# Three reorderings in a fused GLA and MLA block: gate sums behind the sixth product, two weight splits sooner, the last head's outputs ahead of the first pair's values

## The chip, the cores and the metric

The kernel runs on one core of a Trainium2 chip. The metric is the device time of one execution in microseconds (us), lower is better. The core has five instruction queues that run on their own and wait for each other by semaphores: TensorE (PE, matmuls; PEld is its loading of weights), VectorE (DVE), ScalarE (ACT), GpSimd (POOL) and SyncE (SP, which here only issues DMAs). Each works through its instructions strictly in order: what stands behind a waiting instruction waits too.

## The reference, cut to what matters

One transformer block over 512 tokens of width 1024, in fp32. One wide projection feeds a gated linear attention (GLA, 4 heads, two directions, chunks of 64) and a latent attention (MLA, 8 heads); both are gated, added, projected, and followed by a squared-ReLU MLP.

```python
n = rmsnorm(h, g_mix[l])
proj = n @ w_in[l]
(gq, gk, gv, gr, z_gf, z_gb, cq, ckv, kr, z_ma, z_mb) = jnp.split(proj, SPLIT_IDX, axis=-1)
y_gla = gla_branch(gq, gk, gv, gr, z_gf, z_gb, w_gate_f[l], b_gate_f[l], w_gate_b[l], b_gate_b[l], g_gla[l])
y_mla = mla_branch(cq, ckv, kr, positions, g_q[l], w_uq[l], g_kv[l], w_ukv[l])
merged = jax.nn.sigmoid(z_ma) * y_gla + jax.nn.sigmoid(z_mb) * y_mla
h = h + merged @ w_out[l]
m = rmsnorm(h, g_mlp[l])
h = h + jnp.square(jax.nn.relu(m @ w_ff1[l])) @ w_ff2[l]
return rmsnorm(h, g_final)
```

z_gf and z_gb (16 columns each) are the inputs of the GLA's two forget gates, kr (32 columns) is the rotated part of the MLA's key, z_mb gates the MLA.

## The kernel before, in words

**Split numbers.** Every product is made in fp32r from operands split into a high and a low half: ACT copies the operand into the rounded type (high, L93), DVE subtracts it from the operand (low, L94), and `mm3` (L87 to L90) issues three matmuls, high by high (L88), high by low (L89) and low by high (L90). Here "gk1h" and "gk1l" are the halves of the weights for gk of head 1. The halves of weights live in pools of four buffers each (tags wh and wl, L213 to L216), so a split writes into the buffer of the fourth split ahead of it and waits until PE has read that. PSUM has two pools of four banks, "mm" and "at" (L77).

**The order of the work.** Up to L1076 (PE: L1077) the order on each engine is the order in which the program issues its instructions (`in_program_order`); behind that a list scheduler orders them, held only by `goes_behind`, which puts the first instruction of one traced stretch behind the last of another on the named engines.

**Products by seven (L586 to L666).** The projections gr and gv (1024 columns each) are made as seven products of half blocks instead of eight, in the order SEVEN = (1, 2, 5, 6, 3, 7, 4). Products 1, 6, 7 and 4 add onto the same two accumulators ("grx", "gvx"), 5 and 3 onto another two ("grz", "gvz"), 2 has its own ("gvw"). Between them ACT copies partial results (L655) or DVE adds them (L658). So after the sixth product of gr (number 7) DVE adds its accumulators to grc, and the seventh (number 4) goes on adding onto them. The loop at L983 walks through the steps of gr and then gv; each step also prepares the weights two steps ahead (right sums at L603, then the split), and for some steps a filler is run behind the product: another small projection.

**The gate inputs.** The filler of step (0, 6), the fourth product of gr, is `z_chunk_run` (L407 to L423): 16 matmuls give z_gf, z_gb and kr in the bank "zk", with the product by the low halves in other partitions. Then the sums: ACT copies half of the bank (L415), DVE adds (L416) and scales into kr (L417), ACT and DVE split the gate inputs into z4 (L418 to L420), and SP issues four copies that build kr and kswap (L421 to L423). z4 is read by `Gates(0)` (L436), behind gv's third product; kr and kswap by `rotary_k` (L826), far behind.

**The stretch behind gr (L1017 to L1041)** is written out by hand: the gate logs, sums and exponentials of head 0 (`Gates`) between gv's last products, then gk of head 1 (`begin_qk(1, 1)` splits its weights, `finish_qk` makes the product), then gv's last product and the gate zb5 (`begin(C_ZB + 5 * P, "zb5")` splits, `finish_zb` makes the product). `gv.sinks(3)` and `gv.sinks(7)` split rows of v (L679, helper L97 and L98).

**The last GLA head and the first pair (L1115 to L1119).** `up_units(0)` (L846) makes the query, key and value of the first two MLA heads: it yields behind the weights, behind uq, behind uk and behind each of two value blocks uv. Then `gla_out` (L692) makes the last GLA head's outputs, 48 matmuls into two "at" banks, `gla_squares` (L707) their squares on ACT and their scale on POOL, `gla_gated` (L717) the gated rows on DVE (L722), which frees the banks. The attention loop (L1122) runs over 32 tiles of scores: scores s (L905), row maximum top (L907), exponential e (L910), scaling by the reciprocal of the sum (L911 to L915), the flip tp on PE (L924), the values av; the next pair's units are strewn among them.

Of the kernel before, what the change touches and what calls it, by code (L numbers as in the profile page):

```python
# [18 lines left out]
P = 128  # L19
# [16 lines left out]
C_ZA, C_ZB = 3776, 4800  # L36
# [20 lines left out]
def tile_block(ctx: ExitStack, tc: tile.TileContext, t, out: bass.AP):  # L57
# [10 lines left out]
    def u2(name, dt=F32, shape=(P, S)):  # L68
        return tl(list(shape), dt, "u2", 29, name)
# [37 lines left out]
    def traced():  # L107
        return len(nc.cur_bb.bb.instructions)
# [12 lines left out]
    PE_ONLY = (mybir.EngineType.PE,)  # L121
    SPLITTERS = (mybir.EngineType.Activation, mybir.EngineType.DVE)

    def goes_behind(late, early, engines):

        ins = nc.cur_bb.bb.instructions
        for e in engines:
            a, b = [[i for i in ins[x:y] if i.engine == e] for x, y in (early, late)]
            if a and b:
                issued_after(b[0], a[-1].name)  # L130
# [259 lines left out]
    def split_gates():  # L390
        for d in ("f", "b"):
            nc.scalar.activation(gates[d], wg_raw[d], AF.Copy)
            nc.vector.tensor_tensor(
                gates[d][64:128, :], wg_raw[d][64:128, :], raw(gates[d][64:128, :]), op=ALU.subtract
            )
# [11 lines left out]
    def z_chunk_run(begun):  # L407
        w, acc = begun
        for k in range(KD):
            for x in range(2):  # L410
                nc.tensor.matmul(
                    acc, w[:, k, :], xT[k][:, x, :], start=k == 0 and x == 0, stop=k == KD - 1 and x == 1
                )
        both = u2("zkl")
        nc.scalar.activation(both[0:64, :], acc[64:128, :], AF.Copy)  # L415
        nc.vector.tensor_tensor(both[0:64, :], acc[0:64, :], both[0:64, :], op=ALU.add)  # L416
        nc.vector.tensor_tensor(kr[0:64, :], both[0:64, :], R[0:64, :], op=ALU.mult)  # L417
        nc.scalar.activation(z4[0:32, :], kr[0:32, :], AF.Copy)  # L418
        nc.vector.tensor_tensor(z4[32:64, :], kr[0:32, :], raw(z4[0:32, :]), op=ALU.subtract)
        nc.vector.tensor_copy(z4[64:128, :], raw(z4[0:64, :]))  # L420
        for a, b in ((32, 48), (48, 32)):  # L421
            nc.sync.dma_start(kswap[a + 32 : a + 48, :], kr[b : b + HALF, :])
            nc.sync.dma_start(kr[a + 32 : a + 48, :], kr[a : a + HALF, :])  # L423
# [268 lines left out]
    def gla_out(h, sc):  # L692

        half, at = h // 2, (h % 2) * GDV
        accs = [ps("at", f"gla{h}o{j}") for j in range(2)]
        c = slice(at, at + GDV)
        os = []
        for i in range(NT):
            o = accs[i // 2][:, (i % 2) * GDV : (i % 2 + 1) * GDV]
            tok = slice(i * P, (i + 1) * P)  # L700
            for j in range(NT):
                mm3(o, sc[j][:, 0, tok], sc[j][:, 1, tok], v[j, half][:, 0, c], v[j, half][:, 1, c],
                    j == 0, j == NT - 1)
            os.append(o)
        return os
# [36 lines left out]
    class Latent:  # L742
# [4 lines left out]
        def begin(self, j):  # L747
            self.begun[j] = proj_begin(w_in, self.col + j * P, f"{self.name}{j}")
# [97 lines left out]
    def up_units(pr):  # L846

        wq = stage(3, P, f"wq{pr}")
        for k in range(3):
            nc.sync.dma_start(  # L850
                wq[:, k, :].rearrange("p (h e) -> p h e", h=2), w_uq[:, k, 2 * pr : 2 * pr + 2, 0:NOPE]
            )
        wqh, wql = halves(3, P, f"wq{pr}")
        split(wqh, wql, wq, nc.gpsimd)
        wk = stage(2, 384, f"wk{pr}")
        nc.sync.dma_start(
            wk.rearrange("p k (h e) -> p k h e", h=2), w_ukv[:, :, 2 * pr : 2 * pr + 2, :]
        )
        wh, wl = halves(2, 384, f"wk{pr}")
        src = wk.rearrange("p k (h e) -> p k h e", h=2)  # L860
        for k in range(2):
            for c, e in ((slice(0, 128), slice(0, NOPE)), (slice(128, 384), slice(NOPE, 192))):
                split(wh[:, k, c].rearrange("p (h e) -> p h e", h=2),
                      wl[:, k, c].rearrange("p (h e) -> p h e", h=2), src[:, k, :, e], nc.gpsimd)
        qs = []
        for i in range(2):
            q = u4(f"q{pr}{i}")
            h = (2 * pr + i) * HALF
            for x in range(2):
                at = NOPE + x * HALF  # L870
                nc.sync.dma_start(raw(q[at : at + HALF]), raw(ro[x][h : h + HALF]))
            qs.append(q)
        yield
        accq = up_T(wqh, wql, cq, f"uq{pr}")
        for i in range(2):
            split_scaled(qs[i][0:64, 0, :], qs[i][0:64, 1, :], accq[i * 64 : i * 64 + 64, :], QK_SCALE)
        yield
        acck = up_T(wh[:, :, 0:128], wl[:, :, 0:128], ckv, f"uk{pr}")
        for i in range(2):
            kb = kbuf[2 * (pr % 2) + i]  # L880
            split(kb[0:64, 0, :], kb[0:64, 1, :], acck[i * 64 : i * 64 + 64, :])
        yield
        vs = []
        for j in range(2):
            acc = ps("mm", f"uv{pr}{j}")
            for i in range(2):
                tok = slice((2 * j + i) * P, (2 * j + i + 1) * P)
                for k in range(2):
                    mm3(acc[:, i * 256 : i * 256 + 256], ckv[k][:, 0, tok], ckv[k][:, 1, tok],
                        wh[:, k, 128:384], wl[:, k, 128:384], k == 0, k == 1)  # L890
            hl = u4(f"v{pr}{j}", F32R, (P, 2, 2, 256))
            split(hl[:, 0].rearrange("p a b -> p (a b)"), hl[:, 1].rearrange("p a b -> p (a b)"), acc)
            vs.append(hl)
            yield
        for i in range(2):
            heads[2 * pr + i] = (qs[i], kbuf[2 * (pr % 2) + i], vs, slice(i * MV, (i + 1) * MV))
# [63 lines left out]
    def begin_qk(h, x):  # L960
        col, name = ((C_GQ, "gq"), (C_GK, "gk"))[x]
        return begin(col + h * P, f"{name}{h}")
# [4 lines left out]
    def finish_zb(f, begun):  # L967
# [3 lines left out]
    fillers = {  # L971
        (0, 2): (lambda: begin(C_ZB + 4 * P, "zb4"), lambda w: finish_zb(4, w)),
        (0, 6): (lambda: z_chunk_begin("mm"), z_chunk_run),
        (1, 2): (lambda: begin_qk(1, 0), lambda w: finish_qk(1, 0, w)),
    }
# [6 lines left out]
    begun = {}  # L982
    for n, (a, m) in enumerate(steps[:-4]):  # L983
        ahead = steps[n + 2]
        if a == 0:
            for x in {3: (0,), 7: (2, 1), 4: (3,)}.get(m, ()):
                sevens[1].load(x)
        if steps[n + 1] in fillers:
            at = traced()
            begun[steps[n + 1]] = fillers[steps[n + 1]][0]()  # L990
            goes_behind((at, traced()), loading, (mybir.EngineType.SP,))
        if n == 1:
            split_sums(x_y, 5, 6)
        if n == 2:
            split_sums(x_z, 7, 3)
        if (a, m) == (0, 5):
            load_gates()
            pos_i = u2("pos_i", I32)
            nc.gpsimd.dma_start(pos_i, t["positions"][0].partition_broadcast(P))
        if (a, m) == (0, 4):  # L1000
            split_gates()
        if (a, m) in fillers:
            sevens[a].product(m)
            sevens[ahead[0]].prepare(ahead[1])
            fillers[a, m][1](begun.pop((a, m)))
        elif m == 7:
            sevens[a].multiply(m)
            sevens[ahead[0]].prepare(ahead[1])
            sevens[a].sinks(m)
        else:  # L1010
            sevens[ahead[0]].prepare(ahead[1])
            sevens[a].product(m)
# [13 lines left out]
    gate.sums("b")  # L1026
    gv.right_sums(4)
    gv.right_split(4, 0)
    gate.exps("b")
    gv.multiply(3)  # L1030
    w_k = begin_qk(1, 1)
    gv.multiply(7)
    near, nxt, far = gla_qk(0, gate.parts)
    gv.right_split(4, 1)
    gv.sinks(3)
    gv.sinks(7)
    w_b = begin(C_ZB + 5 * P, "zb5")
    finish_qk(1, 1, w_k)
    gv.product(4)
    w_a = begin_za(0)  # L1040
# [2 lines left out]
    for h in range(GH - 1):  # L1043
        sc = gla_scores(near, nxt, far)
        gate = Gates(h + 1)
        gate.logs()
        w_b = begin_za(2 * h + 1)
        acc = proj_run(w_a, xT)
# [10 lines left out]
        os = gla_out(h, sc)  # L1059
# [3 lines left out]
        if h < 2:  # L1063
            w_b = begin_qk(h + 2, 1)
# [14 lines left out]
    h = GH - 1  # L1079
# [16 lines left out]
    sc = gla_scores(near, nxt, far)  # L1096
# [3 lines left out]
    at = traced()  # L1100
# [8 lines left out]
    at = traced()  # L1109
# [2 lines left out]
    ro = rotary_q()  # L1112
    goes_behind((mid, traced()), (at, mid), PE_ONLY)
    g2.append(gated(proj_run(zb, xT, None, range(3, KD)), "b7")[1])
    for _ in up_units(0):  # L1115
        pass
    os = gla_out(h, sc)
    rs = gla_squares(h, os)
    gla_gated(h, os, rs)  # L1119
    LAG_B, LAG_C = 3, 6  # L1120
    units = iter(())
    for n in range(4 * MH + LAG_C):  # L1122
        if n % 8 == 1 and n // 8 + 1 < MH // 2:
            units = up_units(n // 8 + 1)
# [107 lines left out]
    begun = rows_product(merged, t["w_out"][0], KD, "wo", first_half_square, normed, flipped)  # L1232
# [256 lines left out]
```

## Time and profile before

| | |
|---|---|
| median of 3 timed runs | 776.53 us (776.03 to 777.01) |
| profiled execution, its own time | 774.47 us |
| its span, first to last instruction | 772.8 us |
| granted TensorE clock, mean | 0.998 |
| instructions | 10152 |
| POOL busy | 117.9 us of the span |
| moved by DMA | 73.94 MB, mean 96 GB/s |

The span is what the trace covers; the profiled execution's own time is 1.67 us longer than it. Lines of the profile name the line of the kernel, the engine, the operation and the tiles (out<-in). In a timeline the first column is the start in us from the span's beginning, the second the duration (for a row "x2" from the first start to the last end), and the bracket at the end is the engine's idle time ahead of the instruction and what ended it. Matmuls overlap: each shows 0.39 us though the next starts earlier, so a loss on PE is read from the distance of starts. In a row of busy time by stretch stand the stretch, its length, then busy time and count of PE, PEld, DVE, ACT and POOL, the granted clock, the DMA engines' share and GB/s. In the list of the costliest groups, after the bar, stand busy time, mean ns of one, and idle time ahead.

### The profile page before, as it was taken

To read this page: it belongs to the slowest core of one execution; us is meant where nothing else is said; L and a number is where in the kernel's file an instruction comes from. 1 tells how busy PE (TensorE), PEld (TensorE's weight loads), DVE (VectorE), ACT (ScalarE), POOL (GpSimd) and SP (SyncE) were. 2 spreads that over 40 slices of the span, in tenths; PEclk is the share of its full clock that TensorE was granted. 3 is DMA by queue.
4 is the path that set the end of the run, shared out by engine and by line. 5 is a ranking of instruction groups with operands and counts; after the bars stand their busy time and mean duration, and the time that the engine had idled before them with its cause. 6 is when DMAs were issued, how large, how long until landed. Compare 5 with 4: busy or idle time off the path is not lost.

```text
span 772.8 us, 10152 instructions
## 1 busy us (share of the span) xinstructions
PE 759.4 (98%) x3768; PEld 640.6 (83%) x3768; DVE 571.3 (74%) x850; ACT 441.8 (57%) x749; POOL 117.9 (15%) x190
## 2 busy tenths in 40 slices
PE   9999899999999999999999999999999999999996
PEld 7888687888898889899888988888888888888885
DVE  7788989665667775899963676965787478848695
ACT  7556657384566555788833465444644465336644
POOL 0710004251615105211110100000000000000014
PEclk9999999999999999999999999999999999999999
DMA  9732301221324516131033731263115510560002
GB/s 315 244 110 82 119 24 28 56 56 55 82 56 103 91 33 150 35 82 55 29 144 101 250 106 55 68 203 111 55 38 182 160 31 28 176 179 1 27 1 109
DMA packets 93185, 73.94 MB, mean 96 GB/s; under 512 B 15088, under 2 KB 74480, under 8 KB 93136
## 3 DMA queue, kind: packets, MB, share of 16 engines
q1 hardware_dynamic: 92048, 70.14, 30.9%
q10 hardware_dynamic: 864, 2.38, 0.8%
q0 software_dynamic: 224, 0.79, 0.3%
q8 instruction: 29, 0.48, 0.3%
q14 instruction: 20, 0.16, 0.1%
HBM read 69.62 MB, written 2.10 MB: 93 GB/s over the span
## 4 chain that ended last, share of the span: by engine, by line
PE 90%; DVE 5%; ACT 2%; issue 1%; POOL 1%; POOLq 0%; ACTq 0%
PE f L89 8%; PE f L88 8%; PE f L90 8%; PE gx L88 4%; PE gx L89 4%; PE gx L90 4%; PE first L325 3%; PE za L88 2%; PE wo L90 2%; PE za L89 2%; PE wo L88 2%; PE gz L88 2%; PE za L90 2%; PE wo L89 2%; PE gz L89 2%; PE gz L90 2%
## 5 line engine op out<-in xcount | busy, mean ns | idle before, releaser
L1428 POOL DMA_DIRECT2D gfin<-in_g_final x1 | 0.7, 653 | 282.7 <-PE f L90 282.7
L1253 DVE TENSOR_TENSOR w<-w,w 128x1024 f32<-128x1024 f32 x32 | 38.7, 1220 | 0.4
L907 DVE TENSOR_REDUCE top<-s 128x1 f32<-128x512 f32 x32 | 21.7, 679 | 5.2 <-PE s L90 5.1
L910 ACT ACTIVATE e<-s,top 128x512 f32<-128x512 f32 x32 | 21.9, 686 | 5.6 <-DVE top L907 2.9
L470 POOL COPY v3f<-rrf 128x4 f32<-128x4 f32 x4 | 2.8, 708 | 140.3 <-DVE rrf L453 140.3
L1200 DVE TENSOR_TENSOR h<-gx,h 128x512 f32<-128x512 f32 x32 | 21.5, 683 | 1.9 <-PE gx L90 1.8
L94 DVE TENSOR_TENSOR pT<-tp,pT 128x512 fp32r<-128x512 f32 x32 | 21.6, 678 | 0.8 <-ACT pT L93 0.7
L93 ACT ACTIVATE pT<-tp 128x512 fp32r<-128x512 f32 x32 | 19.0, 595 | 4.0 <-PE tp L924 3.8
L942 POOL TENSOR_TENSOR tb<-tb,za 128x512 f32<-128x512 f32 x8 | 11.2, 1402 | 54.8 <-DVE tb L941 40.5
L924 PE MATMUL tp<-ident,e 128*128 128x128 f32 x128 | 19.2, 272 | 0.0
L88 PE MATMUL av<-pT,v 128*128 128x256 f32 x64 | 19.1, 299 | 0.0
L89 PE MATMUL av<-pT,v 128*128 128x256 f32 x64 | 18.5, 289 | 0.0
L1306 ACT ACTIVATE fa<-f 128x512 f32<-128x512 f32 x32 | 18.5, 577 | 0.0
L924 PEld LDWEIGHTS tp<-ident,e 128*128 128x128 f32 x128 | 15.5, 140 | 3.5 <-PE s L90 0.6
L90 PE MATMUL av<-pT,v 128*128 128x256 f32 x64 | 18.2, 285 | 0.0
L93 ACT ACTIVATE gbh<-y 128x512 fp32r<-128x512 f32 x16 | 10.1, 634 | 14.0 <-DVE y L1323 14.0
L94 DVE TENSOR_TENSOR sc<-sc,sc 128x512 fp32r<-128x512 f32 x16 | 10.9, 690 | 9.5 <-ACT sc L93 9.5
L93 ACT ACTIVATE sc<-sc 128x512 fp32r<-128x512 f32 x16 | 9.3, 595 | 11.5 <-DVE sc L541 11.5
L88 PE MATMUL s<-kbuf,q 96*128 96x512 f32 x32 | 14.0, 437 | 1.2 <-DVE grb L722 0.9
L93 ACT ACTIVATE b_10h<-w 128x1024 fp32r<-128x1024 f32 x7 | 7.4, 1060 | 12.1 <-PE gz L90 6.0
L93 ACT ACTIVATE b_20h<-w 128x1024 fp32r<-128x1024 f32 x7 | 7.4, 1059 | 12.1 <-PE gz L90 6.0
L93 ACT ACTIVATE b_00h<-w 128x1024 fp32r<-128x1024 f32 x7 | 7.4, 1057 | 12.1 <-PE gz L90 6.0
(1569 smaller groups left out, 2885.7 us busy)
## 6 DMA issues: line engine op xcount, KB each, us to landing
w<-in_w_ff SPq DMA_DIRECT2D x64, 256.0 KB, 3.4
grw<-in_w_in SPq DMA_DIRECT2D x8, 512.0 KB, 8.6
gvw<-in_w_in SPq DMA_DIRECT2D x8, 512.0 KB, 4.5
x<-in_xt SPq DMA_DIRECT2D x8, 256.0 KB, 5.2
vw<-in_w_first SPq DMA_DIRECT2D x8, 256.0 KB, 5.3
h<-in_x ACTq DMA_DIRECT2D x4, 512.0 KB, 5.4
out<-ms SPq DMA_DIRECT2D x7, 256.0 KB, 2.2
q<-ro SPq DMA_DIRECT2D x16, 64.0 KB, 2.3
```

What stands on the lines that cost most here:

```text
L88: nc.tensor.matmul(acc, lh, rh, start=start, stop=False, skip_group_check=onto)
L89: nc.tensor.matmul(acc, lh, rl, start=False, stop=False, skip_group_check=onto)
L90: nc.tensor.matmul(acc, ll, rh, start=False, stop=stop, skip_group_check=onto)
L93: nc.scalar.activation(hi, src, AF.Copy)
L94: rest.tensor_tensor(lo, src, raw(hi), op=ALU.subtract)
L325: nc.tensor.matmul(f_accs[i], a[:, i * P : (i + 1) * P], b, start=k == 0 and x == 0, stop=k == KD - 1 and x == 2)
L907: nc.vector.tensor_reduce(top, acc, axis=AX.X, op=ALU.max, negate=True)
L910: nc.scalar.activation(e, acc, AF.Exp, bias=top, accum_out=tot)
L924: nc.tensor.transpose(tp[:, k * P : (k + 1) * P], e[:, k * P : (k + 1) * P], ident)
L1200: nc.vector.tensor_tensor(hc, acc, hc, op=ALU.add)
L1253: nc.vector.tensor_tensor(wq[dst][g], wq[x][g], wq[y][g], op=op)
L1306: nc.scalar.activation(a, acc, AF.Relu)
```

## The change

`z_chunk_run` is cut in two: the matmuls stay the filler behind the fourth product, the sums (`z_chunk_finish`) are issued at the top of step (0, 4), that is behind the sums of the sixth product and ahead of the split of the gate weights (`split_gates`). The split of gk's weights moves ahead of `gate.exps("b")`, that of zb5's weights ahead of `gv.sinks(3)`. The outputs of the last GLA head are traced behind the third unit of the first pair, and the two value blocks are held behind them on PE.

```diff
                 nc.tensor.matmul(
                     acc, w[:, k, :], xT[k][:, x, :], start=k == 0 and x == 0, stop=k == KD - 1 and x == 1
                 )
+        return acc
+
+    def z_chunk_finish(acc):
         both = u2("zkl")
         nc.scalar.activation(both[0:64, :], acc[64:128, :], AF.Copy)
...
         if (a, m) == (0, 4):
+            z_chunk_finish(z_acc)
             split_gates()
         if (a, m) in fillers:
             sevens[a].product(m)
             sevens[ahead[0]].prepare(ahead[1])
-            fillers[a, m][1](begun.pop((a, m)))
+            rest = fillers[a, m][1](begun.pop((a, m)))
+            if (a, m) == (0, 6):
+                z_acc = rest
...
     gv.right_split(4, 0)
+    w_k = begin_qk(1, 1)
     gate.exps("b")
     gv.multiply(3)
-    w_k = begin_qk(1, 1)
     gv.multiply(7)
     near, nxt, far = gla_qk(0, gate.parts)
     gv.right_split(4, 1)
+    w_b = begin(C_ZB + 5 * P, "zb5")
     gv.sinks(3)
     gv.sinks(7)
-    w_b = begin(C_ZB + 5 * P, "zb5")
     finish_qk(1, 1, w_k)
...
-    for _ in up_units(0):
+    units = up_units(0)
+    for _ in range(3):
+        next(units)
+    at = traced()
+    os = gla_out(h, sc)
+    values = traced()
+    for _ in units:
         pass
-    os = gla_out(h, sc)
+    goes_behind((values, traced()), (at, values), PE_ONLY)
     rs = gla_squares(h, os)
     gla_gated(h, os, rs)
```

In the built program the number of instructions on every engine is the same. On PE nothing moves ahead of the swap at the last head; behind it the scheduler also puts the third score tile ahead of the uq product of the second pair and shifts a few instructions of the attention loop against each other on every engine. On SP the four copies of kr and kswap come behind three more loads for gv and the load of zb5's weights; the query copies of the second pair come behind the loads of the fourth pair's weights.

## The prediction

> **What bounds the kernel now.** I read the page's list of engines first, then the waits of TensorE (PE), then busy time by stretch.
>
> ```profile
> PE 759.4 (98%) x3768; PEld 640.6 (83%) x3768; DVE 571.3 (74%) x850; ACT 441.8 (57%) x749; POOL 117.9 (15%) x190
> ```
>
> PE is busy for 759.4 of 772.8 us. No other engine is near that, so a change that adds no arithmetic can only give back PE's idle time: 13.4 us in all. Its waits (columns: us in total, times, longest):
>
> ```profile
> PE grx L88 <- DVE grc L658: 2.7, 1, 2.7
> ...
> PE s L88 <- DVE grb L722: 0.9, 1, 0.9
> PE gk L90 <- DVE gk1l L94: 0.5, 1, 0.5
> PE zb L90 <- DVE zb5l L94: 0.4, 1, 0.4
> PE gk L88 <- ACT gk1h L93: 0.3, 1, 0.3
> ```
>
> These five are 4.8 us, and the three edits lie exactly at them. The rest of the idle time is at the start and the end, which no edit touches. Two stretches matter for what comes behind:
>
> ```profile
> 150.00:280.00 130.00, 130.00 (x700) 112.13 (x699) 86.86 (x158) 77.38 (x126) 41.53 (x81) 1.00 0.29 69
> ```
>
> ```profile
> 320.00:390.00 70.00, 69.69 (x480) 62.73 (x479) 66.14 (x131) 59.70 (x128) 12.62 (x12) 1.00 0.19 54
> ```
>
> From 150 to 280 us PE has no idle time and VectorE (DVE) is busy for 86.86 of 130 us, so time won before 150 shifts this stretch as a whole. From 320 to 390 us DVE is busy for 66.14 of 70 us: the stretch in which a gain could be lost again.
>
> **Edit 1: the sums of the gate inputs behind the sixth product.** The seventh product of gr adds onto the two accumulators that the sixth has just filled, so it must wait until DVE has read them (grc, L658). DVE is late because the gate sums stand ahead of it.
>
> ```profile
> 72.75 1.06 ACT L93 ACTIVATE gr71h<-grw 128x1024 fp32r<-128x1024 f32 x1
> ...
> 74.99 0.68 DVE L416 TENSOR_TENSOR zkl<-zk,zkl 64x512 f32<-64x512 f32 x1
> ...
> 75.45 0.39 PE L90 MATMUL grz<-gr31h,xs 128*128 128x512 f32 x1
> ...
> 79.37 1.22 DVE L94 TENSOR_TENSOR gr41l<-grw,gr41h 128x1024 fp32r<-128x1024 f32 x1
> ...
> 80.21 0.39 PE L90 MATMUL grx<-gr71h,xs 128*128 128x512 f32 x1
> ...
> 80.89 0.39 PE L90 MATMUL grx<-gr71h,xs 128*128 128x512 f32 x1
> ...
> 83.19 1.28 DVE L658 TENSOR_TENSOR grc<-grx,grc 128x512 f32<-128x512 f32 x2
> ...
> 84.03 0.47 PE L88 MATMUL grx<-gr40h,xT 128*128 128x512 f32 x1 [2.75 <-DVE grc L658]
> ```
>
> Matmuls of this shape start 0.227 us apart (80.89 less 80.21 is three of them). So PE lost 84.03 - 80.89 - 0.23 = 2.9 us here. In the changed kernel gr41h on ScalarE (ACT) no longer stands behind the z sums, but its buffer (a pool of four, L214) was last gr31h's, read until 75.45 + 0.39 = 75.84. It then takes 1.06 us (as gr71h), and gr41l starts at 76.9. From there grc follows after 83.19 - 79.37 = 3.82 us, at 80.7; the first accumulator is complete at 80.21 + 0.39 = 80.60, just ahead of it. PE goes on 84.03 - 83.19 = 0.84 us later, at 81.6. That is **2.4 us** sooner; 0.5 us of the wait stays, since this read can't go away. Ends: 2.6 if only the sixth product's end decides, 1.4 if gr41h comes 1 us later still.
>
> The moved work isn't gone. The four DVE operations with their pause for ACT ran from 74.99 to one split (1.2) ahead of 79.37, 3.2 us, and now stand behind grc, so DVE is 3.2 - 2.4 = 0.8 us later than before when it reaches gv20l, while PE is 2.4 earlier. What covers that are DVE's own waits between 84 and 147 us:
>
> ```profile
> DVE gv51l L94 <- ACT gv51h L93: 0.7, 1, 0.7
> DVE gv31l L94 <- ACT gv31h L93: 0.4, 1, 0.4
> DVE gv21l L94 <- ACT gv21h L93: 0.4, 1, 0.4
> ...
> DVE gv61l L94 <- ACT gv61h L93: 0.3, 1, 0.3
> DVE mf L439 <- ACT l L437: 0.3, 1, 0.3
> DVE gq1l L94 <- ACT gq1h L93: 0.3, 1, 0.3
> ```
>
> and the low half of gv2 (first row) against its first reader (second):
>
> ```profile
> 89.30 1.23 DVE L94 TENSOR_TENSOR gv20l<-gvw,gv20h 128x1024 fp32r<-128x1024 f32 x1
> ...
> 95.25 0.39 PE L89 MATMUL gvw<-gv20l,xT 128*128 128x512 f32 x1
> ```
>
> Each ends with an ACT copy that itself waits for PE to release a buffer or finish a sum, so with PE earlier they shrink. The two at gv21l and gq1l (0.7) take up the 0.8: from there DVE is as before. The other four (1.7 us, with the steps between them up to 2.2) then put DVE about 2.0 us ahead at the gate logs. gv20l is next late: it was done at 90.53, 4.7 us ahead of its first reader at 95.25, and has 4.7 - 2.4 - 0.8 = 1.5 us left. ACT's z copy now waits for kr with gate_f, gate_b and gv20h queued behind it; DVE does kr ahead of the gates' halves and gv20l, so this delay lies inside the same margin. The zk bank is read some 10 us later, behind grc and the four operations that follow it, and still ahead of the gv2 product, the next to take accumulators from that pool. On SP's queue the four copies of kr and kswap go behind three gvw loads and zb5f, which no longer stand behind them; they wait for kr with only za0f queued behind, and their rows are used at the rotation of k, 200 us later: cost nothing.
>
> **Edit 2: two weight splits sooner.**
>
> ```profile
> 125.77 1.23 DVE L94 TENSOR_TENSOR gv40l<-gvw,gv40h 128x1024 fp32r<-128x1024 f32 x1 [0.19 <-ACT gv40h L93]
> ...
> 127.89 0.39 PE L90 MATMUL gvx<-gv71h,xs 128*128 128x512 f32 x1
> ...
> 128.56 1.23 DVE L94 TENSOR_TENSOR gk1l<-gk1f,gk1h 128x1024 fp32r<-128x1024 f32 x1 [0.36 <-ACT gk1h L93]
> ...
> 129.84 0.50 PE L90 MATMUL gk<-xT,gk1l 128*128 128x512 f32 x1 [0.53 <-DVE gk1l L94]
> ...
> 135.69 2.12 DVE L98 SCALAR_TENSOR_TENSOR gv<-gvb,r_x,gv 128x512 fp32r<-128x512 f32 x2
> ...
> 139.78 1.63 DVE L94 TENSOR_TENSOR zb5l<-zb5f,zb5h 128x1024 fp32r<-128x1024 f32 x1
> ...
> 140.63 0.39 PE L89 MATMUL zb<-xT,zb5h 128*128 128x512 f32 x1
> ...
> 141.47 0.50 PE L90 MATMUL zb<-xT,zb5l 128*128 128x512 f32 x1 [0.45 <-DVE zb5l L94]
> ```
>
> From the last gvx matmul at 127.89 to the first that reads gk1l at 129.84 PE makes three steps, which unhindered take 0.68 us: it lost 1.3, with the slow restart behind it (as below) **1.4**. At zb it lost 141.47 - 140.63 - 0.23 = 0.6, with a restart of 0.50 for 0.39 us **0.7**. With PE 2.4 earlier, gk's third matmul, the first that needs gk1l, is due at 127.89 + 3 x 0.23 - 2.4 = 126.2. DVE reaches gv40l at 125.77 - 2.0 = 123.8, and gk1l now follows it at once, not 2.8 us behind: start 124.9, end 126.1. It fits with almost nothing to spare; if DVE is only 1.5 ahead, 0.4 us is lost. Without the move it would end at 127.8, so this edit also keeps what edit 1 wins. zb5l goes ahead of the four gv operations (135.69 to 139.78): about 133.4 to 135.0, needed at 140.86 - 2.4 - 1.4 = 137.1, so 2 us of cover. What is queued behind the two splits (gvb, gvc, the exponentials for b, gv) is 1.2 us or 1.6 us later against its neighbours, and its first readers, the scores and the outputs of head 0, come behind gk, the last gv product and zb, 16 us of matmuls. I take the whole 2.1 us; ends 1.0 and 2.1.
>
> **Edit 3: the last head's outputs ahead of the first pair's values.** The same matmuls in another order.
>
> ```profile
> 299.76 0.28 PE L88 MATMUL uv<-wk0h,ckvhl 128*128 128x256 f32 x1
> ...
> 302.63 0.28 PE L88 MATMUL gla3o<-gv,sc 128*128 128x256 f32 x1
> ...
> 310.71 0.40 PE L89 MATMUL uq<-cqhl,wq1h 128*128 128x512 f32 x1
> ...
> 311.11 0.88 DVE L722 SCALAR_TENSOR_TENSOR grb<-gla3o,gla3ss,grb 128x256 f32<-128x256 f32 x2 [1.14 <-POOL gla3ss L714]
> ...
> 312.05 0.50 PE L88 MATMUL s<-kbuf,q 96*128 96x512 f32 x1 [0.94 <-DVE grb L722]
> ...
> 315.86 0.60 PE L924 MATMUL tp<-ident,e 128*128 128x128 f32 x4
> ```
>
> ```profile
> L907 DVE TENSOR_REDUCE top<-s 128x1 f32<-128x512 f32 x32 | 21.7, 679 | 5.2 <-PE s L90 5.1
> L910 ACT ACTIVATE e<-s,top 128x512 f32<-128x512 f32 x32 | 21.9, 686 | 5.6 <-DVE top L907 2.9
> ```
>
> The outputs start 302.63 - 299.76 = 2.87 us sooner, and with them squares, GpSimd's (POOL) three operations and grb, now at 311.11 - 2.87 = 308.2, done at 309.1. The third score tile waited for grb's bank and lost 312.05 - 310.71 - 0.23 = 1.1 us. The built order puts it ahead of five uq matmuls (1.2 us), so it is due at 310.94 - 1.2 = 309.8: free by then, with 0.7 us to spare. Next late is the first softmax: grb, grc (0.88 a pair) and two value splits (0.6 to 0.7 each by L416's row) now stand on DVE ahead of the first row maximum, which starts at about 311.2. Three maxima (0.68 each by L907), a reciprocal and then ACT's scaling (0.7 by L910) end at about 314.5; the flip of this tile is due at 315.86 - 1.1 = 314.8. POOL's three operations pass ahead of wk2l, whose readers come with the third pair, and the first out-product load waits behind wk2l for its buffer, with 70 us in hand. I take **1.0 us**; ends 1.1 and, if the maxima hold PE up, -0.5. The scheduler also shuffles the loop up to 390 us; PE loses 0.31 us there now, and I put 0 for this, ends -1 and +0.3.
>
> **Sum.** 2.4 + 1.4 + 0.7 + 1.0 = 5.5 us. The profiled execution took 774.47 us, 1.67 around its span, and would take 769.0. The median of the timed runs is 776.53, 2.06 above it; I take the same 5.5 from the median: **771.0 us**.
>
> [...] By the idle column alone, less the 0.5 that stays, the sum would be 4.3 us, and the time 772.2.
>
> **Rivals.**
> - *Given back at gk.* DVE and ACT, not PE, set the pace from 84 to 142 us. For: DVE's work is the same, only later, and gk1l arrives with nothing to spare. Against: DVE's six waits above. If DVE gains nothing on the way, gk1l ends at 128.2, PE loses 2.0 of the 5.5: 773.0 us.
> - *Edit 3 idle.* The third tile gets its bank, but the flip waits for the late first softmax: gain 4.5 or a little less, 772.0 to 772.6 us.
> - *The edit doesn't move the wait.* If weights of gr4 or gv1 and not grc released the seventh product, edit 1 wins about 0 and edit 2 still 2.1: 773 to 774 us.
> - *Slower.* In the attention loop of 32 score tiles DVE has 3.9 us free in 70. If the new order makes PE wait for DVE once in every tile, the loop decides: from 5.5 / 32 = 0.17 us a tile on, the change is a loss; at 0.25 us it costs 8 us, 779.0 us. Against: the loop's work is the same and DVE enters it about 1 us earlier than before.
>
> **How the numbers follow.** Forecast (gain 4.8 to 6.2) 0.57; edit 3 idle 0.16; given back at gk or the wait not moved 0.15; a gain under 1.6 us 0.06; slower by the loop 0.06. The range leaves out the last two and a little of the third: from 776.53 - 6.2 = 770.3, with 0.5 for the spread of the runs (776.03 to 777.01), 769.8 below; above 773.7 with the same 0.5, 774.2. About 0.2% (1.55 us) is what a measurement of this kernel can tell from no change. Faster by more 0.88, within 0.06, slower 0.06.
>
> **What would show it.** PE's wait for grc at 0.3 to 0.7 us, with the seventh product at about 81.6 us; no wait at gk and zb; the first score matmul of head 0 (bd, L523) 4.3 to 4.6 us earlier than now; no wait of s for grb, and PE idle under 0.6 us from 310 to 390. A wait at gk over 1 us shows the first rival, a wait of tp behind e the second. Waits of a few tenths at many tiles of s or tp would make the prediction wrong.

## The result, and the profile after

The changed kernel takes 769.32 us (median of 4 runs, 769.10 to 769.52), the kernel before 776.43 in the same comparison: ratio 0.9908, with an interval of 0.9891 to 0.9925. It is 7.1 us faster, where 5.5 were forecast, and lies 0.5 us below the range (769.8 to 774.2). Its profiled execution took 769.4 us with a span of 767.7, 5.1 less than the span of 772.8 that the prediction worked from. So the prediction was right against the execution that it was worked out from, and wrong against the timed runs. To read what follows one must know that executions of the kernel before take either about 774.5 us (8 of 71 in the runs below) or 775.6 to 777.1 us (the other 63, the median among them); the one profiled first was a short one.

PE's row of the list of engines, and all its waits (the changed kernel):

```profile
PE 758.5 (99%) x3768; PEld 641.4 (84%) x3768; DVE 571.4 (74%) x850; ACT 441.8 (58%) x749; POOL 119.1 (16%) x190
```

```profile
PE warm L315 <- POOL ident masks.py:199: 1.5, 1, 1.5
PE grx L88 <- DVE grc L661: 0.4, 1, 0.4
PE s L88 <- ACT e L913: 0.3, 1, 0.3
PE s L88 <- DVE pT L94: 0.2, 1, 0.2
```

The wait for grc is 0.4 instead of 2.7 us; those for gk1l, gk1h, zb5l and grb are gone, one of 0.3 us for e is new, and PE is idle for 9.2 us of the span instead of 13.4. The timeline of the changed kernel around the places of edits 1 and 2 (the starts are to be read 0.15 us earlier against those of before, since its first product ran 0.15 us later):

```profile
76.10 1.06 ACT L93 ACTIVATE gr41h<-grw 128x1024 fp32r<-128x1024 f32 x1 [1.20 <-PE grz L90]
77.20 1.23 DVE L94 TENSOR_TENSOR gr41l<-grw,gr41h 128x1024 fp32r<-128x1024 f32 x1 [0.85 <-ACT gr41h L93]
...
81.04 1.28 DVE L661 TENSOR_TENSOR grc<-grx,grc 128x512 f32<-128x512 f32 x2
...
81.87 0.47 PE L88 MATMUL grx<-gr40h,xT 128*128 128x512 f32 x1 [0.42 <-DVE grc L661]
...
124.94 1.22 DVE L94 TENSOR_TENSOR gk1l<-gk1f,gk1h 128x1024 fp32r<-128x1024 f32 x1
...
126.39 0.40 PE L90 MATMUL gk<-xT,gk1l 128*128 128x512 f32 x1
...
133.27 1.63 DVE L94 TENSOR_TENSOR zb5l<-zb5f,zb5h 128x1024 fp32r<-128x1024 f32 x1
```

gr41h waits for PE's last read of its buffer, as the prediction had it, and the seventh product begins at 81.87 (81.72 on the old scale; predicted 81.6). gk1l ends at 126.16, 0.23 us ahead of its first reader.

### The profile page after: what moved, and what is told of

Same layout as the page of the kernel before. It is cut to its first block, busy times and chain, and to the rows that moved or that the text cites. A ratio compares the mean times of both kernels' runs of the same rounds, so it can differ in the third digit from the quotient of the medians.

```text
span 767.7 us, 10149 instructions
## 1 busy us (share of the span) xinstructions
PE 758.5 (99%) x3768; PEld 641.4 (84%) x3768; DVE 571.4 (74%) x850; ACT 441.8 (58%) x749; POOL 119.1 (16%) x190
## 4 chain that ended last, share of the span: by engine, by line
PE 96%; DVE 2%; ACT 1%; issue 0%; POOL 0%; POOLq 0%; ACTq 0%
PE f L89 8%; PE f L90 8%; PE f L88 8%; PE gx L88 4%; PE gx L89 4%; PE gx L90 4%; PE first L325 3%; PE za L88 2%; PE za L89 2%; PE wo L89 2%; PE wo L90 2%; PE gz L89 2%; PE za L90 2%; PE gz L88 2%; PE wo L88 2%; PE gz L90 2%
```

## The experiments

The theory at the start (A): the edits win what the first trace shows, 5 us, and the other 2 us are a difference between executions that no edit touches. The rival (B): one of the removed waits is 2 us longer in the long executions than in the one that was profiled first. The first four runs were to tell them apart.

**The kernel before, unchanged.**

> The kernel before, unchanged, as a run of its own. The first profiled execution took 774.47 us (span 772.8), the four timed runs 776.03 to 777.01. Theory A (the edits win what the profile shows, about 5 us, and the other 2 us of the measured 7.1 are a difference between executions of the kernel before): executions of it spread from 774.4 to 777, and a profile of a longer one shows the 2 us somewhere that no edit touches (start, loads, end). Theory B (in the longer executions one of the removed waits is longer than in the one first profiled): a longer execution has its span 2 us longer too, and PE's wait for grc, gk1l, zb5l or grb is 2 us longer than the 2.7, 0.5, 0.4 and 0.9 of the first profile.

776.12 us (774.45 to 777.05, beside one execution of 1280.68 with a mean granted clock of 0.557, which is left out of the comparison and stays unexplained), ratio 0.9995 (0.9986 to 1.0004). Its profile is of a long execution, 776.33 us with a span of 774.6, and the waits are the old ones within 0.1 us. What differs stands in the row of busy time by stretch, just behind PE's wait for grc; the column behind POOL's is the granted clock:

```profile
84.00:85.00 1.00, 0.73 (x3) 0.62 (x4) 1.00 (x3) 1.00 (x2) 0.00 (x0) 0.80 1.05 403
85.00:86.00 1.00, 1.00 (x4) 0.81 (x3) 1.00 (x2) 1.00 (x3) 0.00 (x0) 0.50 1.14 321
86.00:87.00 1.00, 1.00 (x4) 0.81 (x3) 1.00 (x2) 0.96 (x2) 0.00 (x0) 0.50 0.99 234
87.00:88.00 1.00, 1.00 (x4) 0.72 (x4) 1.00 (x2) 0.00 (x0) 0.00 (x0) 0.50 0.00 0
88.00:89.00 1.00, 1.00 (x6) 0.83 (x5) 0.97 (x3) 0.07 (x1) 0.00 (x0) 1.00 0.00 0
```

The same stretch in the execution that the prediction was worked out from:

```profile
85.00:86.00 1.00, 1.00 (x6) 0.80 (x5) 1.00 (x2) 1.00 (x3) 0.00 (x0) 1.00 1.17 320
86.00:87.00 1.00, 1.00 (x6) 0.83 (x5) 1.00 (x2) 0.72 (x2) 0.00 (x0) 1.00 0.66 156
```

Both show PE fully busy: busy time says nothing here, but four matmuls a microsecond instead of six, and a clock of 0.50, do. The lost clock, (0.20 + 3 x 0.50) / 0.50, makes 3.4 us at half speed. In the timeline of the long execution the distances are 0.43 instead of 0.227 us:

```profile
84.27 0.48 PE L88 MATMUL grx<-gr40h,xT 128*128 128x512 f32 x1 [2.76 <-DVE grc L658]
...
85.40 0.63 PE L88 MATMUL grx<-gr40h,xT 128*128 128x512 f32 x1
85.83 0.63 PE L89 MATMUL grx<-gr40l,xT 128*128 128x512 f32 x1
86.25 0.63 PE L90 MATMUL grx<-gr40h,xT 128*128 128x512 f32 x1
```

So theory A was wrong in the very place where it was sure. B missed too, by the sign that it had named, since no wait is longer; but the loss does hang on a removed wait: behind the wait for grc the clock falls to half in this long execution.

**Edit 1 alone** (the other two left out):

```diff
+        return acc
+
+    def z_chunk_finish(acc):
         both = u2("zkl")
...
         if (a, m) == (0, 4):
+            z_chunk_finish(z_acc)
             split_gates()
```

> Edit 1 alone (gate sums behind the sixth product). By the profile of the changed kernel the wait for grc falls by 2.3 us; without the earlier split of gk1l the logs and gk1l move only with DVE, about 2.0 us, so PE then waits longer at gk and the gain at the scores is 2.0 to 2.2 us. Theory A: 774.2 us where before gives 776.4. Theory B, if the wait for grc is the one that varies: 772.2.

772.73 us, ratio 0.9949 (0.9937 to 0.9962): 3.8 us, between the two expectations and nearer to B. The clock is 1.00 up to the last matmul; the wait for grc is 0.4, and those at gk are 0.5 and 0.5 where before had 0.5 and 0.3.

**Edit 2 alone.**

```diff
+    w_k = begin_qk(1, 1)
     gate.exps("b")
     gv.multiply(3)
-    w_k = begin_qk(1, 1)
...
+    w_b = begin(C_ZB + 5 * P, "zb5")
     gv.sinks(3)
     gv.sinks(7)
-    w_b = begin(C_ZB + 5 * P, "zb5")
```

> Edit 2 alone (splits of gk and zb5 sooner). The waits at gk (1.4 us by starts) and zb (0.7) go: gain 2.1 us, with PE's wait for grc unchanged at 2.7. Theory A: 774.3 us where before gives 776.4. Theory B, if gk or zb vary: 772.3.

774.62 us, ratio 0.9975 (0.9964 to 0.9986): 1.9 us. The waits at gk and zb are gone, that for grc is 2.7, and the clock falls to 0.50 behind it.

**Edit 3 alone.**

```diff
-    for _ in up_units(0):
+    units = up_units(0)
+    for _ in range(3):
+        next(units)
...
+    os = gla_out(h, sc)
...
+    goes_behind((values, traced()), (at, values), PE_ONLY)
```

> Edit 3 alone (last head's outputs ahead of the first pair's values). By the changed kernel PE wins 1.3 us up to the first flip and loses 0.4 up to the end of the attention loop: gain 0.9 us. Theory A: 775.5 us where before gives 776.4. Theory B, if the wait for grb is the one that varies: 773.5.

775.72 us, ratio 0.9986 (0.9976 to 0.9996): 0.85 us; clock at 0.50 behind the wait, as in before.

A profile of one execution separates the parts better than the times, if it is read from the end of the first product, since the start before it varies by up to 1 us (28.1 to 29.2 us in these kernels). The four rows are the last matmuls of that product, the last matmul of gr's seventh product, the first scores of head 0, and the first flip. The long execution of before:

```profile
27.40 1.07 PE L325 MATMUL first<-xT,first3h 128*128 128x512 f32 x4
...
91.19 0.39 PE L90 MATMUL grx<-gr41h,xT 128*128 128x512 f32 x1
...
148.41 1.05 PE L523 MATMUL bd<-qkb 128*128 128x128 f32 x8
...
317.70 0.60 PE L924 MATMUL tp<-ident,e 128*128 128x128 f32 x4
```

Edit 1 alone:

```profile
28.09 1.07 PE L325 MATMUL first<-xT,first3h 128*128 128x512 f32 x4
...
87.98 0.39 PE L90 MATMUL grx<-gr41h,xT 128*128 128x512 f32 x1
...
145.40 1.05 PE L526 MATMUL bd<-qkb 128*128 128x128 f32 x8
...
314.63 0.60 PE L927 MATMUL tp<-ident,e 128*128 128x128 f32 x4
```

The changed kernel:

```profile
27.31 1.07 PE L325 MATMUL first<-xT,first3h 128*128 128x512 f32 x4
...
87.17 0.39 PE L90 MATMUL grx<-gr41h,xT 128*128 128x512 f32 x1
...
142.31 1.05 PE L526 MATMUL bd<-qkb 128*128 128x128 f32 x8
...
310.39 0.60 PE L927 MATMUL tp<-ident,e 128*128 128x128 f32 x4
```

The same rows of the other profiles give these distances (us):

| kernel | end of first product to start of gr's last matmul (grx) | from there to bd | from bd to tp |
|---|---|---|---|
| before, short execution | 61.13 | 57.23 | 169.27 |
| before, long execution | 62.72 | 57.22 | 169.29 |
| edit 1 | 58.82 | 57.42 | 169.23 |
| edit 2 | 62.77 | 55.08 | 169.28 |
| edit 3 | 62.72 | 57.25 | 168.00 |
| all three | 58.79 | 55.14 | 168.08 |

Each column answers to one edit (all are distances of starts, but for the end of the first product). Edit 1 is worth 2.3 us against the short execution and 3.9 against the long one; the 1.6 between them are the half clock. Edit 2 is worth 2.1, edit 3 is worth 1.2.

**The wait filled with dead matmuls.** If the idle time lowers the clock, matmuls without a use in its place should bring 1.6 us or more.

```diff
             sevens[a].multiply(m)
+            if a == 0:
+                fill = ps("mm", "fill")
+                for _ in range(10):
+                    nc.tensor.matmul(fill, xT[0][:, 0, 0:P], xT[1][:, 0, :], start=True, stop=True)
             sevens[ahead[0]].prepare(ahead[1])
```

> The kernel before with ten matmuls of 128x512 more, whose result nobody reads, in PE's wait for grc (10 x 0.227 = 2.3 us of the 2.75); nothing else is moved, grc ends when it ended. Clock theory (the long executions of before lose about 1.6 us because the granted clock falls to 0.50 for some 3.4 us behind this idle time): the seventh product starts at most 0.2 us later than in before, the clock stays at 1.00 from 84 to 90 us, and the median falls by 1.5 to 2.0 us, to 774.6, with little spread. Rival (the missing 1.6 us has nothing to do with the idle time at grc; it lies with DVE's lateness or elsewhere): 776.5 us as before, or a little more, with the clock at 0.50 near 86 us in most executions.

774.48 us (774.36 to 775.13, 8 runs) against 776.41, ratio 0.9973 (0.9963 to 0.9983). A kernel with ten matmuls more is 1.9 us faster. Its timeline and its busy time by stretch:

```profile
81.40 2.43 PE L1011 MATMUL fill<-xT,xT 128*128 128x512 f32 x10
...
84.33 0.47 PE L88 MATMUL grx<-gr40h,xT 128*128 128x512 f32 x1 [0.51 <-DVE grc L658]
```

```profile
85.00:86.00 1.00, 1.00 (x6) 0.81 (x5) 1.00 (x2) 1.00 (x3) 0.00 (x0) 1.00 1.13 331
86.00:87.00 1.00, 1.00 (x6) 0.80 (x5) 1.00 (x2) 1.00 (x2) 0.00 (x0) 1.00 1.03 245
```

The seventh product starts when it always did (84.33), DVE ends when it always did, the clock stays at 1.00, and all 8 runs are short ones.

**Five and two of them** (`range(5)`, `range(2)`), 1.63 and 2.29 us left idle.

> As the fill of ten, with five such matmuls: 1.1 us of the wait filled, 1.6 us left idle. Clock theory with a limit on the idle time between 0.9 us (the waits at gk and grb, behind which no run showed a lower clock) and 2.75 us: 774.6 if 1.6 us of idle time is short enough, 776.5 if it isn't; a median between, with runs at both times, if the chance falls with the length. Rival (the idle time doesn't matter): 776.5.

> The kernel before with two dead matmuls in the wait for grc, as in the fills of five and ten: about 2.3 us left idle, between the 1.6 us that never cost more than itself and the 2.75 us that mostly does. If there is a sharp limit below 2.3: 776.4 in nearly all runs; if above: 774.6 in all; if the chance depends on where the idle time falls against a window of its own in which the clock is decided: runs at both times, fewer at 776.4 than with 2.75 us (34 of 38 so far).

With five, 774.68 us (774.25 to 775.22), ratio 0.9978 (0.9969 to 0.9988): none of 9 runs is a long one (the longest is the profiled one, with the clock at 1.00 up to its last matmul; its first product ended 0.65 us later than in the short execution of before). With two, 776.24 us, ratio 0.9997 (0.9986 to 1.0009): 5 of 12 runs between 774.44 and 774.60, 7 between 776.18 and 777.09. So the share of long executions fell with the length of the idle time: 63 of 71 at 2.75 us, 7 of 12 at 2.29, 0 of 9 at 1.63. Runs at both times came, as the third case of the expectation has them; the window that this case supposes was the author's guess, and no run shows why the same wait isn't followed by the half clock every time.

**The wait brought back into the changed kernel.** Four DVE operations that leave grc as it is, ahead of the sums of the sixth product:

```diff
             elif m in (2, 3, 7):
+                if m == 7 and self.name == "gr":
+                    for i in range(4):
+                        c = self.c22[i % 2]
+                        nc.vector.tensor_tensor(c, c, c, op=ALU.max)
                 for acc, c in zip(accs, {2: self.c11, 3: self.c12, 7: self.c22}[m]):
```

> The changed kernel with four DVE operations more (each replaces grc's own third tile by the maximum of itself and itself, so nothing of the result changes) just ahead of grc: some 2.4 to 2.7 us of work, so that PE waits for grc about 2.8 us again. Clock theory: the median rises by the wait and by the slow stretch behind it, 2.4 + 1.6 = 4.0, to about 773.3, with the clock at 0.50 for about 3.4 us behind the wait in most executions and perhaps a few near 771.7. Rival (the wait costs only its own length): 771.7 throughout, the clock at 1.00.

773.32 us (771.68 to 774.56, 5 runs), 4.0 more than the changed kernel; one run at 771.68, where the wait alone would put it. PE's wait, and the busy time by stretch behind it:

```profile
PE grx L88 <- DVE grc L665: 2.8, 1, 2.8
```

```profile
84.00:85.00 1.00, 0.73 (x2) 0.66 (x3) 1.00 (x3) 0.84 (x2) 0.00 (x0) 0.71 0.00 0
85.00:86.00 1.00, 1.00 (x4) 0.71 (x4) 1.00 (x2) 0.97 (x2) 0.00 (x0) 0.50 0.00 0
86.00:87.00 1.00, 1.00 (x4) 0.81 (x3) 1.00 (x2) 0.11 (x1) 0.00 (x0) 0.50 0.00 0
87.00:88.00 1.00, 1.00 (x5) 0.77 (x4) 1.00 (x2) 0.00 (x0) 0.00 (x0) 0.58 0.00 0
```

Again 3.4 us at half clock, (0.29 + 0.50 + 0.50 + 0.42) / 0.50, and here with no DMA traffic beside it, so the traffic of 234 to 403 GB/s in the rows of before isn't the cause. With the fill this shows the mechanism from both sides: idle time taken from before, idle time given to after.

**Edits 1 and 2.**

```diff
+            z_chunk_finish(z_acc)
...
+    w_k = begin_qk(1, 1)
...
+    w_b = begin(C_ZB + 5 * P, "zb5")
```

> Edits 1 and 2 together, without edit 3. By the single edits as measured (3.84 and 1.95) the gain is 5.8, and since edit 1 alone left 1.0 us of waits at gk where before had 0.8, up to 0.3 more: 770.3 to 770.8. Rival (edit 1's gain over the predicted 2.4 is an accident of the executions, the predicted terms 2.4 and 2.1 hold): 772.0.

770.13 us, ratio 0.9921 (0.9907 to 0.9934): 6.3 us, just under the expected range, and not the 772.0 of the prediction's two terms.

**The changed kernel again.**

> The changed kernel unchanged, beside the next ones on the same chip. Clock theory (PE's longest wait behind the start is now 0.4 us, nothing lowers the clock): 769.3 us with a spread of a few tenths, none of the steps of 1.6 us that the times of before show. Rival (the executions of any version differ by up to 2 us): a spread of 2 us here too.

769.32 us (769.09 to 769.65), ratio 0.9915 (0.9899 to 0.9932). The step of 2 us between executions is gone.

**The last wait for grc taken away.** The sixth and the seventh product of gr (numbers 7 and 4, by which the expectation calls them) are written one accumulator after the other, and the gates of grb come later:

```diff
+            order = [(p, rb) for p in range(KD // 2) for rb in range(2)]
+            if self.name == "gr" and m in (7, 4):
+                order.sort(key=lambda at: at[1])
+            for p, rb in order:
...
             sevens[ahead[0]].prepare(ahead[1])
+            if a == 0:
+                sevens[a].sinks(3)
             sevens[a].sinks(m)
```

> The changed kernel with the seventh and fourth products of gr written one accumulator after the other, so that DVE reads the first one while the second is still filled, and with the gates of grb put off behind the splits of gv1, so that DVE is free to read by then. The last wait for grc (0.42 us, and the 0.12 us by which the restart is slow) goes: the fourth product's first matmul starts 0.23 us after the last of the one ahead. Expected 0.4 to 0.6 us less than the changed kernel, 768.7 to 768.9 us; if grb's later gates hold up gv20l or what is behind it, a new wait takes it back: 769.3.

770.47 us (770.12 to 771.00), ratio 0.9931 (0.9916 to 0.9946): 1.15 us slower than the changed kernel, worse than either expectation, though the wait for grc is gone and the seventh product ends 58.11 us behind the first product, not 58.79. Its timeline, three rows of DVE and one of PE:

```profile
79.64 0.68 DVE L663 TENSOR_TENSOR grc<-grx,grc 128x512 f32<-128x512 f32 x1
81.59 0.69 DVE L663 TENSOR_TENSOR grc<-grx,grc 128x512 f32<-128x512 f32 x1 [1.27 <-PE grx L90]
...
126.11 1.22 DVE L94 TENSOR_TENSOR gk1l<-gk1f,gk1h 128x1024 fp32r<-128x1024 f32 x1
...
127.39 0.50 PE L90 MATMUL gk<-xT,gk1l 128*128 128x512 f32 x1 [0.71 <-DVE gk1l L94]
```

DVE stands idle for 1.27 us between the two reads, and 45 us later gk1l is 1.17 us behind that of the changed kernel (124.94; 0.11 of it is the later end of the first product) and late for PE: from the end of the first product to bd it is 114.90 us, against 113.93 in the changed kernel, so that PE loses 1.7 us on this way after the 0.7 that it had won.

**That idle time of DVE filled, and gk ahead of gv4.**

```diff
                     nc.vector.tensor_tensor(c, acc, c, op=ALU.add)
+                    if m == 7 and self.name == "gr" and c is self.c22[0]:
+                        self.sinks(3)
...
+    w_k = begin_qk(1, 1)
     gv.right_split(4, 0)
-    w_k = begin_qk(1, 1)
```

> As the version with the accumulators one after the other, but with the gates of grb between DVE's two reads of grc, where DVE had stood idle for 1.27 us, and with the split of gk ahead of the first split of gv4. If that idle time of DVE, carried along to gk (gk1l 1.17 us later, 0.71 us of wait and the restart there), is what made that version 1.15 us slower than the changed kernel: no wait at grc and none at gk, 0.4 to 0.6 us less than the changed kernel, 768.7 to 768.9 us. If the loss comes from somewhere else in the new order of the products: 770 us or more. If only the gate moves and the reads stay late: 769.3 us with the wait of 0.4 us back at grc.

768.76 us (768.12 to 769.48, 4 runs), ratio to before 0.9897 (0.9880 to 0.9913). All PE waits that are left:

```profile
PE warm L315 <- POOL ident masks.py:199: 1.5, 1, 1.5
PE s L88 <- ACT e L917: 0.3, 1, 0.3
PE s L88 <- DVE pT L94: 0.2, 1, 0.2
```

The gate logs (mf), which DVE makes ahead of the moved split, start 83.74 us behind the end of the first product, against 84.95 in the version above and 83.88 in the changed kernel: filling the idle time was enough to take DVE's lateness away. The distance from the end of the first product to bd is 113.19 us, 0.74 less than in the changed kernel. The times of this version and of the changed kernel overlap (769.09 to 769.65 in 8 runs), so 0.6 us of gain is what the trace and the medians say, not what the times alone settle.

## Why the prediction was right and wrong, point by point

**The failed step: "I take the same 5.5 from the median".** Set against its own execution the sum gave 769.0, and the changed kernel takes 769.3 to 769.4. The other 2.06 us, by which the median lay above that execution, were carried through the change as if they were no part of it. They were: 1.6 us of them are the half clock behind the wait that edit 1 removes. The rest is the start (the first product ended 0.24 us later in the long execution) and scatter. The clue lay open: two times of the same program, 774.5 and 776.5, ask which stretch differs between the executions, and one profile can't answer that. The prediction neither priced this nor made the lower end of its range reach to it (776.53 - 6.2 - 0.5); with 1.6 us for "the gap goes with the wait" the range would have begun at 768.2.

**Edit 1** was sized at 2.4 and wins 2.3 in an execution like the one it was worked out from, and 3.9 in the common one. The path was right step by step: gr41h at its buffer's release, grc predicted at 80.7 and found at 80.9 on the old scale, the seventh product 0.1 us late. The moved work was absorbed as argued: the gate logs (mf) started 2.0 us sooner, at 112.26 instead of 114.23.

**Edit 2**: 2.1 us predicted, 2.1 measured. That it "also keeps what edit 1 wins" is shown: alone, edit 1 leaves 1.0 us at gk instead of 0.8. "Almost nothing to spare" is shown by the version in which gk1l came 1.06 us later (from the end of the first product) and PE lost 1.7 us up to bd: the rival "given back at gk" is a real mechanism, from which 0.23 us kept this change away.

**Edit 3**: 1.0 predicted, 1.2 up to the first flip. The wait of s for grb is gone, and the flip starts on time. The loop gives back 0.4 us of it: from the first to the last flip 71.34 us pass (310.39 to 381.73) instead of 70.94 (315.86 to 386.80), inside the ends of -1 and +0.3. Neither the rival "edit 3 idle" nor "slower by the loop" came about.

**The signs.** bd came 4.4 us sooner (142.31 instead of 146.59, and 0.15 for the later start; named were 4.3 to 4.6). PE was idle for 0.63 us from 310 to 390, just over the 0.6 that was named, 0.34 of it in the new wait of s for e.

**The sum in the end**: 2.3 + 1.6 + 2.1 + 1.2 - 0.4 = 6.8 of the measured 7.1 us; the 0.3 left are within the scatter of the start.

By the idle column alone, 4.8 us of waits, the prediction had a time of 772.2; by the distances between starts the same waits are 2.9 + 1.4 + 0.7 + 1.1 = 6.1 us. These were the better measure of PE's loss: their terms came out within 0.2 us each, and PE's idle time fell by 4.2 us where the span fell by 5.1. But even distances, taken from one execution, missed the half clock.

## What to carry to other kernels

Where the timed runs lie some tenths of a per cent above the profiled execution, ask for a profile of a typical run before carrying a sum over to the median: the difference can sit in the very wait that an edit removes. TensorE's waits of 2.29 and 2.75 us could be dearer than their length here, by a stretch of half clock behind them (3.4 us where a profile shows it); filling the wait of 2.75 us down to 1.63 us with useless matmuls was enough to win the clock back in all 9 runs. Of the 1.27 us of idle time put into VectorE's queue 1.06 us were still there 45 us on, at the next place where TensorE waits for it: an idle microsecond there had to be priced at that place.

## What the runs showed of the hardware

- Idle time of TensorE of 2.75 us was followed by 3.4 us at a granted clock of 0.50 in 63 of 71 executions, 2.29 us in 7 of 12, 1.63 us in none of 9 (judged by the times; at 2.29 us the mean granted clock is 0.995 or 0.996 in the 7 and 0.998 in the 5 others; the slow stretch itself is seen in the profiled executions). At a clock of 0.50 matmuls of 128x512 start 0.43 us apart instead of 0.227, which cost 1.6 us here.
- Four profiles show the half clock behind grc: the long execution of before, edit 2, edit 3 and the wait brought back, with waits of 2.76, 2.71, 2.73 and 2.83 us. The clock that they lost, over 0.50, makes 3.40, 3.42, 3.40 and 3.42 us. The short execution of before had a wait of 2.75 us too, and its clock stayed at 1.00; no run shows what sets the two apart.
- Behind the last matmul the clock falls to 0.50 too: in the short execution of before at 769.16 us, 3.26 us after the start of that matmul, in the changed kernel at 763.66 us, 2.83 us after it. The rows of the fall, in this order:

```profile
769.00:770.00 1.00, 0.00 (x0) 0.00 (x0) 0.00 (x0) 0.00 (x0) 0.00 (x0) 0.58 0.93 336
```

```profile
763.00:764.00 1.00, 0.00 (x0) 0.00 (x0) 0.75 (x1) 0.72 (x1) 0.01 (x1) 0.83 0.83 307
```

- The end of the first product varied from 28.1 to 29.2 us between executions of kernels that are the same up to there; this scatter of 1 us is larger than the gain of edit 3 in the times (0.85 us). Most of it is there within the first matmuls of 128x512: the fifth starts 1.2 us after the first in the short execution of before (4.96 to 6.13), 1.5 in the long one (5.0 to 6.5) and 1.8 with edit 3 alone (5.2 to 7.0), where four steps of 0.227 us make 0.91, and the first product ends at 28.23, 28.47 and 29.19 us. The clock column reads 1.00 there in both executions of before, so at the start only the distances show it.
